# When a two-layer decoder trunk computes its modulation rows: less in the second mixer, more in the feed-forwards

## The chip, the core and the metric

The kernel runs on one core of a Trainium2 chip. A core has five engines with a queue each: PE (TensorE, matrix multiplication, fed by PEld, its weight load), DVE (VectorE), ACT (ScalarE), POOL (GpSimd) and SP (SyncE), which here issues almost every transfer. Each engine takes its queue in order. The metric is the time of one execution on the device in microseconds (us), the median of several runs; lower is better.

## What is computed

A decoder trunk of two layers on 256 tokens of width 2048, in float32. Each layer has a mixer (sliding-window attention beside an RWKV-7 recurrence), an output projection, a LayerNorm, a SwiGLU feed-forward and another LayerNorm. All of it is modulated by six rows per layer, which depend on the conditioning vector `c` alone:

```python
cond = jax.nn.silu(c)
for l in range(DEPTH):
    mod = (jnp.einsum('bd,de->be', cond, w_ada[l]) + b_ada[l]).reshape(B, N_MOD, 1, D_MODEL)
    sh_m, sc_m, gt_m, sh_f, sc_f, gt_f = [mod[:, i] for i in range(N_MOD)]
    u = x * (1 + sc_m) + sh_m
    proj = u @ w_in[l]
    ...            # attention and RWKV-7 groups -> y_attn, y_rwkv
    mix = jnp.concatenate([y_attn, y_rwkv], axis=-1) @ w_out[l]
    x = layer_norm(DEEPNORM_ALPHA * x + gt_m * mix, ln1_w[l], ln1_b[l])
    u = x * (1 + sc_f) + sh_f
    gate, up = jnp.split(u @ w_gate_up[l], 2, axis=-1)
    ffn = (jax.nn.silu(gate) * up) @ w_down[l]
    x = layer_norm(DEEPNORM_ALPHA * x + gt_f * ffn, ln2_w[l], ln2_b[l])
```

A layer's modulation weights `w_ada` are 2048 x 12288 floats, 100 MB: a large part of everything that is read.

## The kernel before

**Weights.** `steps` streams a weight matrix in tiles `raw` of 128x1024 floats (512 KB, four buffers). ACT casts each to `hi`, DVE makes the remainder `lo = raw - hi` (L381; three buffers of `hi`, two of `lo`), and PE multiplies three times: twelve matmuls with 512 columns for a tile in `stream` (L402, L403, L405), or 24 with 256 in `tstream` (L414 to L416).

**Modulation rows.** They are computed on DVE. Two rows of the first layer come at the start; the other ten rows are cut into halves of 1024 columns, 20 half rows in a fixed order, and the generator `ada_steps` computes one in 19 steps: 16 steps each load a tile `ast` (512 KB, two buffers, L253) and add it to `aacc` with one DVE instruction (L255 for the first, L257 for the others); two steps (`LAG`) do nothing; the last sums over partitions (`ada_sums`: eight transposes on PE, L277, and eight sums on ACT, L281). One half row follows another. The six half rows ahead of the second layer's `gt_m` are used by the first layer; the last ones, the second layer's `sc_f`, `sh_f` and `gt_f`, are needed in its feed-forward.

**When a step is taken.** After every weight tile `pump` adds the stage's pace to a counter and takes a step for each whole unit. The recurrence (`recur`, L803 and following) takes `AR` steps ahead of each of its four chunks, each attention operation (a, b, c) takes `AA`. `need` takes all steps that are still missing when a row is used. The paces are per layer: `AP` in the mixer, `AO` in the output projection and up to the first f block of the feed-forward, `AF_` from the second f block on and through the next layer's `front`.

```python
    def pump():
        pace[1] += pace[0]
        while pace[1] >= 1.0:
            pace[1] -= 1.0
            next(ada_rest, None)
...
            for cc in range(NCH):
                adv(AR[l])
...
    for l in range(L):
        pace[0] = AP[l]
```

**The mixer's order.** `ORDER` lists its operations: for four groups of head pairs D (decays), R (projection, `tstream`), A (`prepare`, ends in the products `aa` and `am`), I (`invert`), C (`recur`), E (`close`); Q0 to Q2 project the attention's inputs (`stream`); a, b, c are attention, w and z the output projection's first half. `invert` is a long chain: DVE's `am` goes to memory (`nscr`), comes back as `nb` to POOL, which solves 16x16 triangles with 30 small instructions (L733, L735), goes to memory again (`tinv`) and back as `tm`; DVE transposes it (`ytr`, L745), and PE's products `m` (L749, L756) follow. All these transfers go through SP's one queue.

**Who sets the order.** The program is written in this order, but a planner (a scheduler with a timeline of its own) places each engine's instructions in its queue. So a changed pace also moves other instructions.

Of the kernel before, what the change touches and what calls it, by code (L numbers as in the profile page):

```python
# [45 lines left out]
LAG = 2  # L46
WB = (4, 3, 2)
RED = 1
AR = (3, 7)
AA = (1, 45)  # L50
AP = (0.65, 0.3)
AO = (1.1, 2.9)
AF_ = (0.75, 0.55)
COEX = (0, 0)
IB = 'cb'
EB = 'cb'
# [11 lines left out]
def hybrid_trunk_kernel(  # L68
# [269 lines left out]
    def adv(n):  # L338
        for _ in range(n):
            next(ada_rest, None)  # L340
# [106 lines left out]
    def diagonal(t, rows, row0=0):  # L447

        a = t[:]
        return bass.AP(a.tensor, a.offset + row0 * CH, [[16 * CH + 16, 16 * NCH], [rows * CH, 16 // rows], [1, 16]])  # L450

# [38 lines left out]
    def mixer(l, us, mixp, feeds):  # L490
# [71 lines left out]
        def have_y(kts):  # L562
            for k in kts:
                if ys[k] is None:
                    yf = pool_of("ysc").tile([P, T], F32, tag="ysc", name="yf", bufs=1)
                    dma(yf, yd[l, k])
                    ys[k] = split_y(yf)
# [192 lines left out]
        def recur(g, st):  # L760
# [45 lines left out]
            for cc in range(NCH):  # L806
                adv(AR[l])
                o = cc * P
# [206 lines left out]
        for op in ORDER[l].split():  # L1015
# [31 lines left out]
            if op[0] in "abc":  # L1047
                adv(AA[l])
        have_y(range(KT))
# [65 lines left out]
    def channel(l, ys, wa, fp):  # L1115
# [55 lines left out]
        def affine():  # L1171

            lw = fp.tile([P, D], F32, tag="lnw", name="lnw", bufs=2)
            dma(lw, ln1_w[l:l + 1, :].to_broadcast([P, D]))
            lb = fp.tile([P, D], F32, tag="lnw", name="lnb", bufs=2)
            dma(lb, ln1_b[l:l + 1, :].to_broadcast([P, D]))
            for t in range(2):
                for q in range(4):
                    o = q * 512
                    zq = z[:, t, o:o + 512]  # L1180
                    V.tensor_mul(zq, zq, lw[:, o:o + 512])
                    V.tensor_add(zq, zq, lb[:, o:o + 512])
                    yield
# [14 lines left out]
        for lo_g, hi_g in ((0, 6), (6, 11)):  # L1198
            hts = []
            for f in range(lo_g, hi_g):  # L1200
# [3 lines left out]
                if f == 0:  # L1204
# [4 lines left out]
                    rows = affine()  # L1209
                    pace[0] = AF_[l]  # L1210
                else:
# [103 lines left out]
    for l in range(L):  # L1315
        pace[0] = AP[l]
        with tc.tile_pool(name=f"mix{l}", bufs=1, reuse_waits="tile") as mp:
            ys, wa = mixer(l, us, mp, feeds)
        pace[0] = AO[l]
        with tc.tile_pool(name=f"ffn{l}", bufs=1, reuse_waits="tile") as fp:  # L1320
# [31 lines left out]
```

## Time and profile before

| | |
|---|---|
| three runs | 2698.06 us median (2688.91 to 2700.31) |
| the profiled execution | 2694.28 us |
| its span, first to last instruction | 2692.6 us |
| mean granted TensorE clock | 0.965 of full |

The profile is of one execution. A row of a group list gives count, busy time and the mean of one; a row of waits names who waited and what ended the wait; a timeline row gives start and duration of one instruction or of several merged ones, and in brackets the engine's idle time ahead of it with what ended it. `L381` is line 381 of the kernel.

### The profile page before, as it was taken

The numbers are of one execution on the slowest core, as the hardware profiler recorded it, in microseconds if no ns is written. First come the engines' busy times: TensorE is split into PE (matmuls) and PEld (weight loads), VectorE is DVE, ScalarE is ACT, GpSimd is POOL, SyncE is SP. The second block draws the span as 40 slices with busy tenths as digits, with TensorE's granted clock in tenths as the row PEclk, the third lists the DMA queues.
The fourth block names the chain that finished last, engine by engine and source line by source line (L and its number), as shares of the span: only waits on it lengthen the run. The fifth ranks groups of instructions, "written<-read, shape, count | busy, mean of one in ns | idle before, by whom it ended". The sixth has DMA issues, their size and how long they took to land.

```text
span 2692.6 us, 41752 instructions
## 1 busy us (share of the span) xinstructions
PE 2501.1 (93%) x15325; PEld 2093.1 (78%) x15325; DVE 1841.0 (68%) x2469; ACT 1188.3 (44%) x2029; POOL 135.0 (5%) x355
## 2 busy tenths in 40 slices
PE   3788998788999999999999999979899999999997
PEld 2687886567888888888889877867688888888887
DVE  6866767979877777777788677555764545545456
ACT  2364452435444444444445544534444444344442
POOL 1002112000000000000000022110000000000000
PEclk9789998899999999999999999989999999999999
DMA  9968668688998888889878586424756656666654
GB/s 315 381 188 253 198 191 238 180 317 296 353 330 309 297 303 312 293 295 308 308 263 304 174 259 188 117 72 144 253 172 188 190 186 196 195 189 189 193 188 149
DMA packets 351999, 637.49 MB, mean 237 GB/s; under 512 B 75894, under 2 KB 142898, under 8 KB 350258
## 3 DMA queue, kind: packets, MB, share of 16 engines
q1 hardware_dynamic: 351794, 634.82, 71.6%
q8 instruction: 120, 1.97, 0.3%
q14 instruction: 85, 0.70, 0.1%
HBM read 622.08 MB, written 12.62 MB: 236 GB/s over the span
## 4 chain that ended last, share of the span: by engine, by line
PE 68%; DMA 8%; DVE 6%; ACT 2%; issue 1%; POOL 1%; SPq 0%; DVEq 0%; POOLq 0%; ACTq 0%
PE acc L403 19%; PE acc L402 19%; PE acc L405 19%; DMA ast<-in_w_ada_dram 3%; DVE aacc L257 2%; PE acc L414 2%; PE acc L415 2%; PE acc L416 2%; DVE lo L381 1%; DMA raw<-in_w_gate_up_dram 1%; PE mb L1225 1%; DMA raw<-in_w_out_dram 1%; DMA yf<-yd 1%; PE mb L277 1%; ACT pr L947 0%
## 5 line engine op out<-in xcount | busy, mean ns | idle before, releaser
L380 ACT CAST hi<-raw 128x1024 fp32r<-128x1024 f32 (+2 forms) x728 | 758.5, 1044 | 1110.8 <-PE acc L405 833.1
L381 DVE TENSOR_TENSOR lo<-raw,hi 128x1024 fp32r<-128x1024 f32 (+2 forms) x728 | 880.2, 1212 | 519.8 <-PE acc L403 347.1
L403 PE MATMUL acc<-lo,u 128*128 128x512 f32 x1568 | 513.4, 395 | 11.9 <-DVE lo L381 11.8
L405 PE MATMUL acc<-hi,u 128*128 128x512 f32 x1568 | 505.8, 391 | 0.0
L257 DVE SCALAR_TENSOR_TENSOR aacc<-ast,cond,aacc 128x1024 f32<-128x1024 f32 x300 | 384.1, 1280 | 127.8 <-DMA ast<-in_w_ada_dram 126.6
L402 PE MATMUL acc<-hi,u 128*128 128x512 f32 x1568 | 457.2, 393 | 0.9 <-ACT u L360 0.5
L403 PEld LDWEIGHTS acc<-lo,u 128*128 128x128 f32 x1568 | 293.8, 189 | 76.4 <-DVE lo L381 16.2
L402 PEld LDWEIGHTS acc<-hi,u 128*128 128x128 f32 x1568 | 294.9, 188 | 63.4 <-ACT sg L1218 0.9
L405 PEld LDWEIGHTS acc<-hi,u 128*128 128x128 f32 x1568 | 295.2, 188 | 61.8 <-issue 0.5
L403 PE MATMUL acc<-lo,ht 128*128 128x512 f32 (+1 forms) x720 | 243.6, 377 | 3.0 <-DVE lo L381 2.9
L405 PE MATMUL acc<-hi,ht 128*128 128x512 f32 (+1 forms) x720 | 242.2, 375 | 0.0
L414 PE MATMUL acc<-u,hi 128*128 128x256 f32 x720 | 206.1, 293 | 14.0 <-ACT hi L380 14.0
L402 PE MATMUL acc<-hi,ht 128*128 128x512 f32 (+1 forms) x720 | 217.0, 376 | 0.0
L415 PE MATMUL acc<-u,hi 128*128 128x256 f32 x720 | 204.5, 291 | 0.0
L416 PE MATMUL acc<-u,lo 128*128 128x256 f32 x720 | 193.1, 294 | 7.1 <-DVE lo L381 7.1
L403 PEld LDWEIGHTS acc<-lo,ht 128*128 128x128 f32 x720 | 135.0, 188 | 29.3 <-DVE lo L381 5.6
L414 PEld LDWEIGHTS acc<-u,hi 128*128 128x128 f32 x720 | 141.9, 197 | 19.3 <-ACT hi L380 14.9
L405 PEld LDWEIGHTS acc<-hi,ht 128*128 128x128 f32 x720 | 135.6, 188 | 24.2
L402 PEld LDWEIGHTS acc<-hi,ht 128*128 128x128 f32 x720 | 134.8, 188 | 24.4
L415 PEld LDWEIGHTS acc<-u,hi 128*128 128x128 f32 x720 | 141.7, 197 | 2.6 <-issue 1.6
L416 PEld LDWEIGHTS acc<-u,lo 128*128 128x128 f32 x720 | 133.8, 197 | 11.6 <-DVE lo L381 9.0
L1067 POOL TENSOR_TENSOR brs<-brs,mhalf 128x1 f32<-128x1 f32 x8 | 7.6, 955 | 1698.7 <-DVE brs L1066 772.1
(349 smaller groups left out, 2901.1 us busy)
## 6 DMA issues: line engine op xcount, KB each, us to landing
ast<-in_w_ada_dram SPq DMA_DIRECT2D x368, 512.0 KB
raw<-in_w_gate_up_dram SPq DMA_DIRECT2D x704, 256.0 KB
raw<-in_w_down_dram SPq DMA_DIRECT2D x176, 512.0 KB
raw<-in_w_in_dram SPq DMA_DIRECT2D x82, 512.0 KB
raw<-in_w_out_dram SPq DMA_DIRECT2D x64, 512.0 KB
raw<-in_w_in_dram SPq DMA_DIRECT2D x120, 256.0 KB
ast<-in_w_ada_dram SPq DMA_DIRECT2D x32, 256.0 KB
lnw<-in_ln_w_dram SPq DMA_DIRECT2D x4, 1024.0 KB
```

Source lines behind the costliest of these rows:

```text
L257: ins = V.scalar_tensor_tensor(acc, t, cond[:, j:j + 1], acc, ALU.mult, ALU.add)
L277: PE.transpose(b[:, i * P:(i + 1) * P], blocks[q + i], ident)
L380: S.copy(h, fl)
L381: ins = V.tensor_tensor(r, fl, h.bitcast(F32), ALU.subtract)
L402: PE.matmul(bt, lhsT=xh, rhs=hi[:, c0:c0 + w], start=st, stop=False)
L403: PE.matmul(bt, lhsT=xh, rhs=lo[:, c0:c0 + w], start=False, stop=False)
L405: PE.matmul(banks[t][q][:, 0:w], lhsT=xl, rhs=hi[:, c0:c0 + w], start=False, stop=sp_)
L414: PE.matmul(bt, lhsT=hi[:, c0:c0 + w], rhs=xh, start=st and opens, stop=False)
L415: PE.matmul(bt, lhsT=hi[:, c0:c0 + w], rhs=xl, start=False, stop=False)
L416: PE.matmul(bt, lhsT=lo[:, c0:c0 + w], rhs=xh, start=False, stop=sp_ and closes)
L1067: G.tensor_tensor(rs[:, 0:1], rs[:, 0:1], mhalf[:, 0:1], ALU.pow)
L1225: PE.transpose(b[:, i * T + t * P:i * T + (t + 1) * P], hh[t][:, (2 * k2 + i) * P:(2 * k2 + i + 1) * P], ident)
```

## The change

Four of the tables that set the steps get other numbers for the second layer, and one for the first (`AF_[0]`); the rest of the kernel is untouched.

```diff
-AR = (3, 7)
-AA = (1, 45)
-AP = (0.65, 0.3)
-AO = (1.1, 2.9)
-AF_ = (0.75, 0.55)
+AR = (3, 0)
+AA = (1, 0)
+AP = (0.65, 0.2)
+AO = (1.1, 0.0)
+AF_ = (0.8, 0.55)
```

In the first layer's feed-forward a step now follows 0.8 of the weight tiles, not 0.75. In the second layer's mixer, no steps are taken in the recurrence and in attention, and one follows every fifth weight tile. What is left is taken from the second feed-forward's second f block on. Up to that point of the first feed-forward the two programs are the same.

Three places of the new order. The first is DVE in the second layer's mixer, between group 0's `am` and the first use of its inversion (`bv` frees the bank of a product, `xr` and `lw` prepare groups 1 and 2). Before:

```order
L381 TENSOR_TENSOR lo<-raw,hi 128x1024
L257 SCALAR_TENSOR_TENSOR aacc<-ast,cond,aacc 128x1024
L381 TENSOR_TENSOR lo<-raw,hi 128x1024
L257 SCALAR_TENSOR_TENSOR aacc<-ast,cond,aacc 128x1024
L720 TENSOR_TENSOR bv<-bnb,vx 128x256
L455 SCALAR_TENSOR_TENSOR xr<-acc,par_132,xr 128x255
L608 TENSOR_SCALAR lw<-lw 128x256 x2
L609 SCALAR_TENSOR_TENSOR lw<-rmask,lw 128x256 x2
```

The same place now:

```order
L381 TENSOR_TENSOR lo<-raw,hi 128x1024 x2
L257 SCALAR_TENSOR_TENSOR aacc<-ast,cond,aacc 128x1024
L720 TENSOR_TENSOR bv<-bnb,vx 128x256
L455 SCALAR_TENSOR_TENSOR xr<-acc,par_132,xr 128x255
L381 TENSOR_TENSOR lo<-raw,hi 128x1024
L608 TENSOR_SCALAR lw<-lw 128x256 x2
L609 SCALAR_TENSOR_TENSOR lw<-rmask,lw 128x256 x2
```

The `aacc` between the `lo` are gone but for one; from there to the end of group 1's inversion no other stands. On PE, 82 matmuls with 512 columns and 44 with 256 stood between group 0's last `aa` and its first `m` (L749), and now 72 and 31; the small products between are the same.

The second place is DVE in the LayerNorm that ends the first feed-forward, behind the last `lo` (`tp`, `z`, `bst`: the two halves' residual and statistics; L1078 writes a half's normalised `z`). Before:

```order
L257 SCALAR_TENSOR_TENSOR aacc<-ast,cond,aacc 128x1024
L1264 TENSOR_TENSOR tp<-acc,gtf 128x512
L1265 SCALAR_TENSOR_TENSOR z<-z,tp 128x512
L1267 BN_STATS bst<-z 128x6
L1064 BN_AGGR bmv<-bst 128x2
L1066 TENSOR_SCALAR brs<-bmv 128x1
L1072 SCALAR_TENSOR_TENSOR brs<-bmv,brs 128x1
L1078 TENSOR_SCALAR z<-z,brs 128x512 x2
L1264 TENSOR_TENSOR tp<-acc,gtf 128x512
L1265 SCALAR_TENSOR_TENSOR z<-z,tp 128x512
L1267 BN_STATS bst<-z 128x6
L1064 BN_AGGR bmv<-bst 128x2
```

Now, behind an `aacc` and the first `tp` that stand ahead as before:

```order
L257 SCALAR_TENSOR_TENSOR aacc<-ast,cond,aacc 128x1024
L1265 SCALAR_TENSOR_TENSOR z<-z,tp 128x512
L1267 BN_STATS bst<-z 128x6
L1064 BN_AGGR bmv<-bst 128x2
L1066 TENSOR_SCALAR brs<-bmv 128x1
L1264 TENSOR_TENSOR tp<-acc,gtf 128x512
L1072 SCALAR_TENSOR_TENSOR brs<-bmv,brs 128x1
L1265 SCALAR_TENSOR_TENSOR z<-z,tp 128x512
L1078 TENSOR_SCALAR z<-z,brs 128x512 x2
L257 SCALAR_TENSOR_TENSOR aacc<-ast,cond,aacc 128x1024
L1267 BN_STATS bst<-z 128x6
L257 SCALAR_TENSOR_TENSOR aacc<-ast,cond,aacc 128x1024
```

Three `aacc` have come into it.

The third place is SP's queue in the second layer's mixer, where attention begins: group 3's inversion (`nscr`, `nb`, `tinv`, `tm`), the last projection's result on its way through memory (`qkv`, `qk`) and weights. Before:

```order
L686 DMA nscr<-am 64x4x64 x4
L727 DMA nb<-nscr 64x16x16 x2
L372 DMA raw<-in_w_out_dram 128x1024 x3
L738 DMA tinv_154<-ttl 64x8x16 x2
L372 DMA raw<-in_w_out_dram 128x1024
L876 DMA qkv<-stg 128x512
L372 DMA raw<-in_w_out_dram 128x1024
L741 DMA tm<-tinv_154 64x8x64
L876 DMA qkv<-stg 128x512
L741 DMA tm<-tinv_154 64x8x64
L888 DMA qk<-qkv 128x2x256
```

Now:

```order
L686 DMA nscr<-am 64x4x64 x2
L727 DMA nb<-nscr 64x16x16 x2
L372 DMA raw<-in_w_out_dram 128x1024
L876 DMA qkv<-stg 128x512
L372 DMA raw<-in_w_out_dram 128x1024
L876 DMA qkv<-stg 128x512
L738 DMA tinv_154<-ttl 64x8x16
L888 DMA qk<-qkv 128x2x256
L889 DMA qk<-qkv 128x2x64
L890 DMA vt<-qkv 128x2x64 x2
L738 DMA tinv_154<-ttl 64x8x16
```

The inversion's `tinv` has come behind both `qkv` and stands around the first `qk`. On PE, 55 matmuls with 512 columns stood between group 3's last `aa` and the projection's end, and now 17.

## Rows read from the trace of the kernel before

**Rows 1.** The page's head: each engine's busy time, share, instructions.

```profile
PE 2501.1 (93%) x15325; PEld 2093.1 (78%) x15325; DVE 1841.0 (68%) x2469; ACT 1188.3 (44%) x2029; POOL 135.0 (5%) x355
```

**Rows 2.** Busy time by stretches: length, each engine's busy us, granted clock, DMA share, GB/s.

```profile
700.00:1390.00 690.00, 684.68 (x3159) 566.71 (x3158) 527.29 (x505) 304.38 (x447) 0.00 (x0) 1.00 0.89 308
...
1540.00:1660.00 120.00, 108.37 (x989) 90.53 (x988) 90.25 (x125) 55.26 (x116) 32.55 (x67) 0.94 0.78 235
1660.00:1760.00 100.00, 100.00 (x1083) 84.61 (x1082) 57.15 (x97) 46.65 (x93) 19.80 (x64) 1.00 0.46 126
1760.00:1860.00 100.00, 82.54 (x790) 62.52 (x789) 59.04 (x191) 42.13 (x129) 4.42 (x6) 0.85 0.21 63
1980.00:2640.00 660.00, 660.00 (x2956) 546.85 (x2955) 336.23 (x313) 275.06 (x285) 0.00 (x0) 1.00 0.61 193
```

**Rows 3.** Waits of PE, 1540 to 1660 us: total us, times, longest.

```profile
PE acc L403 <- DVE lo L381: 7.5, 2, 5.3
PE ab L599 <- DVE e L611: 3.0, 1, 3.0
```

**Rows 4.** Timeline of DVE: two of its three longest waits for `ast`.

```profile
1568.95 1.28 DVE L257 SCALAR_TENSOR_TENSOR aacc<-ast,cond,aacc 128x1024 f32<-128x1024 f32 x1 [4.93 <-DMA ast<-in_w_ada_dram]
...
1650.65 1.28 DVE L257 SCALAR_TENSOR_TENSOR aacc<-ast,cond,aacc 128x1024 f32<-128x1024 f32 x1 [6.86 <-DMA ast<-in_w_ada_dram]
```

**Rows 5.** Waits of SP's queue, 1540 to 1670 us.

```profile
SPq L738 <- POOL el L614: 8.4, 1, 8.4
```

**Rows 6.** Stretches of 10 us; the last three columns are clock, DMA share, GB/s.

```profile
1590.00:1600.00 10.00, 10.00 (x122) 9.43 (x122) 7.98 (x12) 6.84 (x24) 0.00 (x0) 0.80 1.02 345
1650.00:1660.00 10.00, 4.68 (x15) 3.71 (x14) 7.71 (x15) 2.35 (x5) 2.57 (x1) 0.66 0.71 194
```

**Rows 7.** Timelines and chain: the inversions of groups 0, 1 and 2.

```profile
1548.76 1.71 PE L681 MATMUL aa<-ar,bkc 64*128 64x128 f32 x16
1563.65 0.44 POOL L733 TENSOR_TENSOR tmp<-nb,ttl 128x15 f32<-128x15 f32 x1 [40.52 <-DMA nb<-nscr]
...
1571.61 1.12 POOL L735 TENSOR_TENSOR ttl<-ttl,tmp 128x30 f32<-128x30 f32 x1
...
1578.95 0.22 POOL L735 TENSOR_TENSOR ttl<-ttl,tmp 128x8 f32<-128x8 f32 x1
...
1588.15 0.71 DVE L745 STREAM_TRANSPOSE ytr<-tm 128x512 f32<-128x512 f32 x1 [0.67 <-DMA tm<-tinv]
1590.25 1.97 PE L749 MATMUL m<-ytr,am 64*64 64x64 f32 x32
...
1668.57 1.08 PE m L749 x32
1674.30 1.09 PE aa L681 x16
1683.45 0.21 POOL L733 TENSOR_TENSOR tmp<-nb,ttl 128x15 f32<-128x15 f32 x1 [24.66 <-DMA nb<-nscr]
...
1694.10 0.22 POOL L735 TENSOR_TENSOR ttl<-ttl,tmp 128x8 f32<-128x8 f32 x1
```

**Rows 8.** Timeline of the first feed-forward's last LayerNorm, DVE and PE.

```profile
1394.36 2.11 DVE L381 TENSOR_TENSOR lo<-raw,hi 128x864 fp32r<-128x864 f32 x2 [0.31 <-ACT hi L380]
...
1406.23 1.53 PE L354 MATMUL mb<-ident,z 128*128 128x128 f32 x6 [4.04 <-DVE z L1078]
```

**Rows 9.** Waits of PE and DVE, 650 to 1400 us.

```profile
PE acc L403 <- DVE lo L381: 6.0, 9, 1.2
...
DVE aacc L257 <- DMA ast<-in_w_ada_dram: 62.2, 52, 3.6
```

**Rows 10.** The chain, where attention begins.

```profile
1760.23 0.25 PE acc L405
...
1769.63 2.32 DMA qk<-qkv
```

**Rows 11.** A stretch of 20 us in the first feed-forward, columns as above.

```profile
720.00:740.00 20.00, 20.00 (x90) 16.53 (x90) 15.98 (x15) 8.34 (x8) 0.00 (x0) 1.00 1.00 370
```

## The prediction

> **What bounds the kernel now.** I read the page's head first: TensorE is busy for 2501.1 us, 93% of the span [rows 1]. That is a mean over unlike stages, so I cut the span into them [rows 2]. The first feed-forward (700 to 1390 us) keeps PE busy 684.68 of 690 us and the second (1980 to 2640) 660 of 660. There only PE's own work counts. The second layer's mixer is different: 108.37 of 120 us in its first part (1540 to 1660), where almost all of its modulation loads lie, 100 of 100 in the next, 82.54 of 100 where attention begins. DVE is busy 90.25 of those 120 us.
>
> Next I read what PE waited for in that first part [rows 3]: DVE's `lo` for 7.5 us in two waits and a bank freed late by DVE for 3.0. DVE's own rows say why it was late [rows 4]: three times, 4.93 us in the first and 6.86 in the last, it stood at the head of its queue on a modulation tile `ast` that had not landed, and the `lo`, `bv` and `e` behind it had to stand too, though they needed nothing of it. The 6.86 us come from SP's queue [rows 5]: its head waited 8.4 us for GpSimd's triangular inversion (`tinv<-ttl`), the `ast` load stood behind that, and DVE got the tile at 1650.65 [rows 4]. After PE's two long gaps the granted clock is below full: 0.80 in the 10 us from 1590, 0.66 in the 10 from 1650 [rows 6].
>
> **What moves.** `pump` runs once per weight tile. From the second f block of the first feed-forward to the end of the next layer's front it runs 80 + 48 + 80 + 40 + 22 = 270 times, so 0.75 to 0.8 adds 13.5, in whole steps 14 (202 to 216). The 20 half rows have 19 steps each (16 loads, LAG 2, one sum), 380 in all, and 138 lie ahead of this stage in both kernels. So the second mixer had 380 - 138 - 202 = 40 steps, of which 28 came from AR (4 x 7 in group 0's recurrence). Now 26 are left, 14 at pace 0.2 in the mixer and 12 in the second feed-forward. In loads, the mixer's 32 become 11; 12 go to the first feed-forward, 9 to the second. AA = 45 and AO = 2.9 found nothing left to give, so their removal does nothing. No load, multiplication or transpose disappears: what can be won is waiting alone.
>
> **Gain: the mixer's first part.** With no `ast` in front of DVE there, the three waits go: 7.5 + 3.0 = 10.5 us [rows 3]. The clock: a mean of 0.94 over 120 us is 14.4 us at the half rate [rows 2], 4.0 of them in the full stretch from 1590; of the 6.8 from 1650 at most 4.68 can have been worked [rows 6]. I take 10 of the 14.4 as worked, which cost half, 5.0, with bounds 2 (after so long a mixer some gap will always come) and 6. Gain 15.5.
>
> **Given back (1): the inversion's latency.** The planner thought DVE full and had put 82 wide and 44 narrow matmuls between group 0's last `aa` and its first `m`; now 72 and 31. By the second feed-forward's pitch (660 us for 2956, 0.22 us, and half of it for a narrow one [rows 2]) that is 3.7 us less cover. The 2.2 and 3.0 us of stall and some 1.7 of the slow clock's cost that also covered the chain are gone: 10.6 us less. The slack was about 0.7 us (`ytr` ends 1588.86, `m` starts 1590.25 [rows 7]). So if the chain stayed as long, PE would wait 9.9 us. But the chain should shrink. From the end of the last `aa` to GpSimd's start it took 13.2 us for group 0, and 8.0 for group 2, which had almost no loads beside it (1550.47 to 1563.65 against 1675.39 to 1683.45 [rows 7]). GpSimd then took 15.5 us (1563.65 to 1579.17) against 10.9 (1683.45 to 1694.32): the same small operation takes 0.22 or 1.12 us [rows 7]. I take 7.5 us of shortening, as weight loads still run: 2.4 us of wait remain, bounds 0 and 9.9. Group 1's `m` came at 1668.57 [rows 7], long after the late `ast` of 1650.65 that its transpose stood behind, so nothing is charged there.
>
> The Trainium skill, SBUF — State Buffer, section "Who interferes with whom", states that a DVE instruction with two SBUF inputs and a GpSimd instruction that reads SBUF block each other for a whole instruction. The trace agrees: the long ones last about as long as a 1.2 us `lo` or `aacc`. By that rule the fewer `aacc` free GpSimd and the wait goes to 0, the sum below to -8.7; with group 0's chain as its rows have it, the wait is 9.9 and the sum +1.2.
>
> **Given back (2): the LayerNorm at the end of the first feed-forward.** The higher pace moves the half row under way: DVE's order now has three more `aacc` between the last `lo` and the last `z` of this LayerNorm. DVE runs there almost without a pause from 1394.36 until PE starts at 1406.23, after 4.04 us on it [rows 8]. Three `aacc` at 1.28 [rows 4] would be 3.84; in the chain rebuilt with the new order some of it falls into DVE's short waits for GpSimd, and the last `z` comes 3.3 us later. Price 3.3 us, bounds 0 (`aacc` slipped into waits) and 6 (a tile that lands late).
>
> **Given back (3): the first feed-forward's body.** Twelve more `aacc` at 1.28 us [rows 4] are 15.4 us on a DVE busy 527 of 690 us [rows 2]. PE there lost 6.0 us in nine waits on `lo`, and DVE waited 62.2 us in 52 waits for `ast` [rows 9]. What hides the additions is the two tiles of `lo` that DVE is ahead. In proportion to the loads that is under 1 us; I take 1.5, bounds 0 and 5. The second feed-forward needs nothing: DVE is busy 336 of 660 us, DMA at 0.61 [rows 2], and a half row's transposes and sums merely move from one full PE stretch to another.
>
> **Given back (4): the start of attention.** In the new order group 3's last `aa` stands 17 wide matmuls ahead of the last projection's end, not 55, and SP's queue puts the first `tinv` ahead of the first `qk` load. Before, `qk` followed the projection's last product by 9.1 us (1760.48 to 1769.63 [rows 10]). Now, from `aa` to the projection's end, 17 wide matmuls take 3.8 us and 38 small ones 2.6 (1.09 for 16 `aa` [rows 7]), so `qk` could start 15.5 us after `aa`; GpSimd, by group 2, ends at 8.0 + 10.9 = 18.9. That is 3.4 us late, partly covered by small products that now fill the same gap: 2.0, bounds -2 and 6.
>
> **Sum.** -15.5 + 2.4 + 3.3 + 1.5 + 2.0 = -6.3. The profiled execution took 2694.28 us (its span of 2692.6 and 1.7 around it): 2688.0. The median shown, 2698.06, lies 3.8 higher, which would give 2691.8; I forecast between the two, **2690**. Its own range is 2683 to 2697. Two runs of this kernel differ by up to 11.4 us, so 0.5% (13.5 us) is about what can be told from no change.
>
> **Rivals.**
> *All is kept:* the chain shrinks fully and the LayerNorm and attention pay nothing: 2694.3 - 15.5 = 2679. For it: the stretch from 1660 to 1760, almost free of loads, has no PE wait at all. Against it: the three `aacc` stand in an unbroken DVE chain.
> *The wait changes its name:* the inversion keeps its length, so 9.9 + 3 us (group 1) come back: -15.5 + 12.9 + 6.8 = +4.2, 2698.5. For it: the 8.4 us that SP waited on GpSimd do not go away by themselves. Against it: group 2.
> *Slower, by the first feed-forward:* there each added step can cost PE its 1.20 us of DVE and the mean wait for its tile, 62.2/52 = 1.20 [rows 9]. It turns the forecast into a loss from three exposed steps of the twelve on; half of them give 2688.0 - 1.5 + 14.4 = 2701, all 2715. For it: while loads run, demand is 1.8 times the weights' own 193 GB/s [rows 2], 347 GB/s, against 338 before. Against it: the twelve loads are 6.3 MB, 20 us at the 308 GB/s of this stage, and its DMA share of 0.89 leaves 76 us of 690 free; and a stretch of 20 us there moved 370 GB/s with PE full throughout [rows 11].
> The Trainium skill, DMA: Bandwidth & Descriptors, section "Where 436 GB/s comes from", gives about 358 GB/s per core as the HBM side's limit; by that rule 347 leaves 3% and hiccups would be paid by PE (an estimate: 17.6 us for the twelve loads, were nothing free). The trace does not bear it out as a limit for one core: that stretch lies above it.
>
> **Chances.** Forecast 0.50, all kept 0.22, wait renamed 0.16, slower 0.12. The range 2676 to 2706 leaves out little more than the far ends of the second and the last. Faster by over 0.5% (below 2684.6): all kept and the forecast's lower edge, 0.26. Slower by over 0.5% (above 2711.5): the last rival's upper part and a term missed, 0.10. Within: 0.64.
>
> **What would show it.** In the new profile: no `aacc` wait of over 3 us between group 0's `aa` and group 1's `m`, and no PE wait on `lo` there; the granted clock at 1.00 in that part; GpSimd's chain of groups 0 and 1 near 11 to 13 us. A PE wait on `ytr` ahead of group 0's `m` measures (1). The wait on `z` at the first feed-forward's end should be near 7 us, not 4. The first feed-forward's PE waits on `lo` should stay below 10 us. The second should be as full as before. I would be wrong if PE's waits there have other owners, a weight tile behind GpSimd in SP's queue above all, or if the planner's new order of other parts costs more than these terms.

## The result, and the profile after

| | median | range, runs |
|---|---|---|
| before | 2693.85 us | 2682.87 to 2700.44, 20 |
| changed | 2701.38 us | 2693.09 to 2711.72, 20 |

The ratio is 1.0029, with a 95% interval of [1.0018, 1.0039]: 5 to 10 us slower, where 8 faster was forecast. That is inside the 0.5% named ahead and inside the range, but on the other side. The profiled executions differ by less, 2692.6 and 2696.7 us of span.

The stretches of [rows 2], now of the changed kernel:

```profile
700.00:1390.00 690.00, 679.13 (x3101) 558.94 (x3100) 531.32 (x500) 302.18 (x449) 0.00 (x0) 1.00 0.90 311
...
1540.00:1660.00 120.00, 117.27 (x1212) 100.67 (x1213) 73.98 (x131) 59.70 (x108) 23.81 (x67) 0.99 0.51 142
1660.00:1760.00 100.00, 99.03 (x989) 83.11 (x987) 55.51 (x85) 48.02 (x94) 13.96 (x43) 1.00 0.55 159
1760.00:1860.00 100.00, 85.40 (x774) 64.61 (x774) 62.53 (x200) 41.46 (x130) 9.70 (x28) 0.85 0.19 58
1980.00:2640.00 660.00, 660.00 (x2960) 546.62 (x2960) 348.13 (x326) 279.25 (x304) 0.00 (x0) 1.00 0.62 200
```

The mixer's first part is what was hoped for: PE 117.27 of 120 us in place of 108.37, the clock 0.99 in place of 0.94. The first feed-forward lost: 679.13 in place of 684.68 us.

Such windows don't move with the program, so I compared the same instruction in both traces: ACT makes the same 784 casts in the same order (L380), and the time from one to another is a stage's length. Casts 140 to 386, counted from 0, are the first feed-forward's body (709.12 to 1388.69 before, 707.65 to 1395.80 now).

| stage (casts) | before | changed | measured | forecast |
|---|---|---|---|---|
| up to cast 140, same program | 709.1 | 707.6 | -1.5 | 0 |
| first feed-forward's body (140 to 386) | 679.6 | 688.2 | +8.6 | +1.5 |
| its LayerNorm (386 to 398) | 29.4 | 31.0 | +1.6 | +3.3 |
| second layer's front (398 to 422) | 83.1 | 85.0 | +1.9 | 0 |
| mixer and attention (422 to 494) | 400.4 | 390.7 | -9.7 | -11.1 |
| output projection, LayerNorm (494 to 518) | 56.1 | 57.2 | +1.1 | 0 |
| second feed-forward's start (518 to 566) | 146.6 | 148.7 | +2.1 | 0 |

The sum is +4.1, the difference of the spans; behind cast 566 nothing moves by more than 0.2. The mixer's gain came nearly as forecast. The first feed-forward took it back.

How much two traces of one program differ can be read from the first row: up to cast 140 all fifteen kernels of this document have the same order of instructions, and that stretch took 703.0 to 715.4 us.

**The first feed-forward.** PE's weight load (PEld) waits for `lo`, 700 to 1396 us, first of the kernel before, then of the changed one:

```profile
PEld acc L403 <- DVE lo L381: 9.9, 13, 1.7
```

```profile
PEld acc L403 <- DVE lo L381: 17.9, 18, 2.1
```

The difference of 8.0 us is nearly the body's loss of 8.6. PE's own rows show less (5.1 and 10.9 us over the same stretch); the ends of matmuls are modelled in this profile. What `lo` is late for stands in DVE's waits and in ACT's (the same stretch, again before and then changed):

```profile
DVE aacc L257 <- DMA ast<-in_w_ada_dram: 62.0, 51, 3.6
ACT hi L380 <- DMA raw<-in_w_gate_up_dram: 18.8, 11, 3.8
ACT hi L380 <- DMA raw<-in_w_down_dram: 11.7, 6, 2.3
```

```profile
DVE aacc L257 <- DMA ast<-in_w_ada_dram: 72.9, 63, 3.9
ACT hi L380 <- DMA raw<-in_w_gate_up_dram: 40.7, 20, 3.8
ACT hi L380 <- DMA raw<-in_w_down_dram: 18.9, 8, 3.0
```

The `ast` waits grew from 62.0 to 72.9 us, and ACT's waits for the weights themselves from 30.5 to 59.6. In both cases there are more waits; the mean `ast` wait stayed at 1.2 us. One such place of the changed kernel, in the timeline of DVE, of ACT and of SP's queue:

```profile
900.66 1.28 DVE L257 SCALAR_TENSOR_TENSOR aacc<-ast,cond,aacc 128x1024 f32<-128x1024 f32 x1 [3.28 <-DMA ast<-in_w_ada_dram]
...
902.99 1.28 DVE L257 SCALAR_TENSOR_TENSOR aacc<-ast,cond,aacc 128x1024 f32<-128x1024 f32 x1
904.19 1.22 DVE L381 TENSOR_TENSOR lo<-raw,hi 128x1024 fp32r<-128x1024 f32 x1
...
910.86 1.28 DVE L257 SCALAR_TENSOR_TENSOR aacc<-ast,cond,aacc 128x1024 f32<-128x1024 f32 x1 [2.79 <-DMA ast<-in_w_ada_dram]
912.06 1.22 DVE L381 TENSOR_TENSOR lo<-raw,hi 128x1024 fp32r<-128x1024 f32 x1
```

```profile
908.29 1.05 ACT L380 CAST hi<-raw 128x1024 fp32r<-128x1024 f32 x1 [1.96 <-DMA raw<-in_w_gate_up_dram]
912.10 1.04 ACT L380 CAST hi<-raw 128x1024 fp32r<-128x1024 f32 x1 [2.76 <-DMA raw<-in_w_gate_up_dram]
```

```profile
904.30 0.33 SPq L253 DMA_DIRECT2D ast<-in_w_ada_dram  x1
905.43 0.80 SPq L372 DMA_DIRECT2D raw<-in_w_gate_up_dram  x2
```

Two kinds of late tile meet: the cast of a weight tile waits for its data, and `lo` stands behind an `aacc` that waits for its own. In the 20 us from 896 PE is busy 17.93.

SP's rows show why the tiles are late: they are asked for late. The `ast` tile that DVE uses at 910.86 was issued at 904.30, as soon as the `aacc` of 902.99 had freed one of the two buffers. The weight tile that is cast at 912.10 was issued at 905.43, as soon as the `lo` of 904.19 had freed one of the four. So it is in the whole body: a load is issued a median of 0.03 us behind the instruction that frees its buffer. Where DVE waits for a modulation tile, it uses the tile a median of 5.2 us after the issue before and 5.25 after the change. Weight tiles that ACT waits for are cast a mean of 5.55 us after theirs before the change and 5.49 after it. The transfers did not become slower. What grew is the number of tiles that DVE is ready for before they land, and such a wait passes through `lo` to the load of the weight tile four further on.

**Its LayerNorm.** PE's wait for the last `z` of [rows 8] went from 4.04 to 4.85, with another of 1.97 ahead of it: 6.8, near the 7 that were named.

```profile
1410.00 0.44 PE L354 MATMUL mb<-ident,z 128*128 128x128 f32 x2 [1.97 <-DVE z L1078]
1415.29 1.54 PE L354 MATMUL mb<-ident,z 128*128 128x128 f32 x6 [4.85 <-DVE z L1078]
```

**Group 0's inversion** [rows 7], GpSimd's first and last instruction, DVE's transpose, PE's wait:

```profile
1562.57 0.21 POOL L733 TENSOR_TENSOR tmp<-nb,ttl 128x15 f32<-128x15 f32 x1 [30.64 <-DMA nb<-nscr]
...
1577.11 0.22 POOL L735 TENSOR_TENSOR ttl<-ttl,tmp 128x8 f32<-128x8 f32 x1
```

```profile
1584.16 0.71 DVE L745 STREAM_TRANSPOSE ytr<-tm 128x512 f32<-128x512 f32 x1 [3.31 <-DMA tm<-tinv]
```

```profile
1584.93 1.73 PE L749 MATMUL m<-ytr,am 64*64 64x64 f32 x32 [2.01 <-DVE ytr L745]
```

The wait is 2.01 us (forecast 2.4). The last `aa` ended at 1554.7, so GpSimd starts 7.9 us behind it (13.2 before, 8.0 forecast) and works 14.8 us (15.5 before; 10.9 in group 2 before).

**The start of attention** [rows 10]: the last projection's matmuls end at 1756.61 and `qk`'s product starts at 1773.25, 16.6 us later; before, it was 13.8 (1760.48 to 1774.28). The difference is 2.8, forecast 2.0.

```profile
1756.22 0.39 PE L405 MATMUL acc<-hi,u 128*128 128x512 f32 x1
...
1773.25 1.37 PE L906 MATMUL acc<-ident,qr 128*128 128x128 f32 x4 [3.34 <-DVE qr L899]
```

**The second feed-forward** now holds a half row's eight transposes, 1.2 us between matmuls on a PE that had no gap:

```profile
2052.60 0.93 PE L277 MATMUL mb<-ident,aacc 128*128 128x128 f32 x7
...
2055.22 0.27 PE L277 MATMUL mb<-ident,aacc 128*128 128x128 f32 x1
```

### The profile page after: what moved, and what is told of

Read it like the earlier page. It is cut to its first block, busy times and chain, and to the rows that moved or that the text cites. A ratio compares the mean times of both kernels' runs of the same rounds, so it can differ in the third digit from the quotient of the medians.

```text
span 2696.7 us, 41738 instructions
## 1 busy us (share of the span) xinstructions
PE 2505.7 (93%) x15325; PEld 2093.7 (78%) x15325; DVE 1841.7 (68%) x2469; ACT 1189.3 (44%) x2029; POOL 125.0 (5%) x355
## 3 DMA queue, kind: packets, MB, share of 16 engines
q8 instruction: 120, 1.97, 0.3%
## 4 chain that ended last, share of the span: by engine, by line
PE 51%; DMA 3%; DVE 3%; ACT 1%; POOL 1%; issue 1%; SPq 0%; DVEq 0%; ACTq 0%; POOLq 0%
PE acc L403 14%; PE acc L402 14%; PE acc L405 14%; PE acc L416 2%; PE acc L414 2%; PE acc L415 2%; DMA ast<-in_w_ada_dram 1%; DVE lo L381 1%; DMA raw<-in_w_out_dram 1%; PE mb L1225 1%; POOL ttl L735 0%; DMA qk<-qkv 0%; DVE aacc L257 0%; PE m L749 0%; DMA raw<-in_w_gate_up_dram 0%
## 5 line engine op out<-in xcount | busy, mean ns | idle before, releaser
L380 ACT CAST hi<-raw 128x1024 fp32r<-128x1024 f32 (+2 forms) x728 | 758.4, 1044 | 1104.0 <-PE acc L405 805.4
L306 DVE SCALAR_TENSOR_TENSOR aacc<-ast,cond,aacc 128x1024 f32<-128x1024 f32 (+1 forms) x75 | 80.3, 1070 | 11.5 <-DMA ast<-in_w_ada_dram 9.9
```

The costliest lines, as they stand in the source:

```text
L306: V.scalar_tensor_tensor(acc, t[:, j], cond[:, j0 + j:j0 + j + 1], acc, ALU.mult, ALU.add)
L380: S.copy(h, fl)
```

## The experiments

The kernels below are the changed one with the edit shown, unless another base is named. "Body" and "mixer" are the stages of the table above, read from one trace of each kernel; the ratio, with its 95% interval, is to the kernel before, and comes from several runs. Three kernels at pace 0.75 (the kernel before and two below) have one order of instructions in the body and took 679.6, 678.9 and 680.2 us there; three at 0.80 have the changed kernel's and took 688.2, 687.0 and 685.4. So less than 3 us between two bodies says little, and the loss is 7.3 us by the means of three.

### Which part costs, which gains

Pace 0.75 kept, the mixer as changed:

```diff
-AF_ = (0.8, 0.55)
+AF_ = (0.75, 0.55)
```

> The change without its higher pace in the first feed-forward (0.75 stays): the second mixer still takes few steps, and the 26 that are left go to the second feed-forward. Theory A (the first feed-forward's extra loads make its weight tiles late, worth about +8 us in its body and +3 to +5 in the LayerNorm and front behind it; the emptier mixer gains about 10): about 10 us faster than the changed kernel and 4 to 9 us faster than the kernel before, no more of PE's waits on lo in the first feed-forward than before (8 us, not 14). Theory B (the emptier mixer gains nothing, because the planner's new order gives all back at the start of attention, and the loss has nothing to do with the pace): as slow as the changed kernel, +5 to +9 us against before.

2698.12 against 2697.31 us, ratio 0.9998 [0.9985, 1.0012]: no change. The body is 678.9 us (before 679.6) and its PEld wait as before, so the loss in the first feed-forward goes with the pace. But the mixer is 399.5 us, hardly shorter than before. Group 0's chain from `aa` to `m` took 30.5 us there, nearly as in the changed kernel (30.3), yet PE waited 5.3 us on `ytr`: the planner had put less other work beside it. That is 3.3 of the 8.9 us between the two mixers; the rest is not traced. Theory A is right on the pace and missed the mixer.

The higher pace alone, on the kernel before:

```diff
-AF_ = (0.75, 0.55)
+AF_ = (0.8, 0.55)
```

> The higher pace in the first feed-forward alone (0.8); the second mixer keeps its tables, and so takes what is left, 26 steps where it had 40. Theory A: the +8 us in the first feed-forward's body and +3 to +5 behind it stand, and the mixer's 14 fewer steps give back a part only: +4 to +10 us against before, PE's waits on lo near 14 us between 640 and 1400. Theory B: the pace costs nothing, 0 to -4 us.

2727.48 us, 1.0104 [1.0087, 1.0122], far worse than either theory had it. The body is 685.4 us (+5.8). Most of the rest is the mixer, 424.1 us: with AR = 7 and only 26 steps left, sixteen `aacc` stand between 1597 and 1646, and group 1's `aa` comes at 1667.92, where it stood at 1608 before. The later groups slip with it, and attention finds group 3's inversion unfinished:

```profile
1667.92 1.16 PE L681 MATMUL aa<-ar,bkc 64*128 64x128 f32 x16
```

```profile
1800.20 0.47 PE L906 MATMUL acc<-ident,qr 128*128 128x128 f32 x1 [10.41 <-DVE qr L899]
```

The change's two halves belong together: under a pace of 0.8 the old mixer tables would have cost 20 us more than the new ones do.

The pace lowered instead:

```diff
-AF_ = (0.8, 0.55)
+AF_ = (0.7, 0.55)
```

> As the change, but the first feed-forward's pace goes down, 0.70 in place of 0.80: 188 steps in place of 216 there, 40 in the second feed-forward. Theory A, if the loss is proportional to the loads: the body gains as much again, 15 to 20 us faster than the changed kernel, 8 to 14 faster than before. Theory A with a threshold (0.75 was still hidden): equal to the kernel with 0.75 and the same tables, within 3 us. Theory B: as the changed kernel.

2686.45 us, 0.996 [0.9945, 0.9976]. The body is 673.3 us (145 tiles, PEld's wait 4.9), the mixer 386.9; the second feed-forward's start costs 6.4 more than before, with 40 steps in it. The body goes on gaining below 0.75, so 0.75 is no threshold: theory A in proportion to the loads.

No step in the mixer at all, pace 0.75:

```diff
-AP = (0.65, 0.2)
+AP = (0.65, 0.0)
-AF_ = (0.8, 0.55)
+AF_ = (0.75, 0.55)
```

> Pace 0.75 in the first feed-forward as before, no step at all in the second mixer, 40 in the second feed-forward (2 of them at once where its rows are needed). Theory A: the last three half-empty loads of the mixer are worth little: within 4 us of the kernel with 0.75 and pace 0.2, so 3 to 10 us faster than before; each half row that goes into the second feed-forward costs about 1 to 3 us there. Theory B: +5 us or more against before.

2681.95 us, 0.9942 [0.9923, 0.996], the best of all: the body 680.2 us, the mixer 381.2, the second feed-forward's start 4.6 longer than before. The mixer is 18 us under that of the kernel with pace 0.2 there, where 4 were expected.

The same with the change's pace:

```diff
-AP = (0.65, 0.2)
+AP = (0.65, 0.0)
```

> The change with pace 0.0 in place of 0.2 in the second mixer: its 14 steps go to the second feed-forward (26 there). It differs from the kernel without mixer steps only by 0.80 for 0.75 in the first feed-forward. If the terms add (body and LayerNorm +10 at 0.80, the mixer without loads 19 us shorter, 2 us for each half row in the second feed-forward): 6 to 12 us slower than that kernel, 3 to 9 faster than before. If the planner's order decides the mixer anew with each shift of the steps: anything from that to slower than before, and the mixer (casts 422 to 494) not within 4 us of 381.

2703.53 us, 1.0026 [1.0012, 1.0039]: as slow as the changed kernel. The body is 687.0 us, as for the other kernels at 0.80 (688.2, 685.4). The mixer has no modulation load in it either, and yet it takes 392.4 us, not 381.2. So a mixer free of loads is not by itself worth 19 us: between 381 and 392 what differs is the planner's order. (The one pair of kernels here that nearly share an order there, two of those below, differ by 2.3 us: 383.7 and 386.0.)

### Bytes or DVE's time

One load of 16 less, DVE's work kept:

```diff
+            if l == 1 and j == 8 and (mod, c0) != (5, 1024):
+                V.scalar_tensor_tensor(acc, acc, cond[:, j:j + 1], acc, ALU.mult, ALU.add)
+                yield
+                continue
```

> The changed kernel without one of the 16 loads of each half row of the second layer (all but the last half row): the step adds the row sum to itself with an instruction of the same length on DVE, so its modulation rows are other numbers. That takes 11 loads of 512 KB away, about as many as the higher pace brings into the first feed-forward, and no instruction of DVE. From the first LayerNorm's end (first transpose of z) to the second's, the kernel before and two others with pace 0.75 took 764.9 to 766.7 us, the two with 0.80 775.5 and 774.3. Theory A1 (the bytes: the weight tiles come later because the engines that move data are full): 765 to 768 here, and ACT's waits for weight tiles near 35 us, not 64. Theory A2 (DVE's time): 774 to 776. In all: A1 about 8 us under the changed kernel, near the kernel before; A2 as the changed kernel, +5 to +10 against before.

2701.04 us, 1.0017 [1.0004, 1.0031]. From LayerNorm to LayerNorm 771.5 us, between the theories; the body 682.9, 5.3 less than the changed kernel and 2.5 less than the shortest body of its order. Lines stand four lower in this kernel:

```profile
PEld acc L407 <- DVE lo L385: 12.9, 17, 1.5
```

All loads, one multiply-add of 16 cut to 32 columns:

```diff
+                w = 32 if l == 1 and j == 8 and (mod, c0) != (5, 1024) else 1024
-                ins = V.scalar_tensor_tensor(acc, t, cond[:, j:j + 1], acc, ALU.mult, ALU.add)
+                ins = V.scalar_tensor_tensor(acc[:, 0:w], t[:, 0:w], cond[:, j:j + 1], acc[:, 0:w], ALU.mult, ALU.add)
```

> The changed kernel with all its loads, but one of the 16 multiply-adds of each half row of the second layer (all but the last half row) works on 32 of the 1024 columns, so its modulation rows are other numbers: about 1.2 us of DVE less, 11 times, and the same bytes. Theory A1 (bytes): still 773 to 776 us from LayerNorm to LayerNorm, +4 to +10 in all against before. Theory A2 (DVE's time): 765 to 769, about the kernel before.

2703.17 us, 1.0035 [1.0017, 1.0053]; the body 688.3, from LayerNorm to LayerNorm 775.5, as the changed kernel:

```profile
PEld acc L404 <- DVE lo L382: 17.6, 22, 1.6
```

Some 12 us less of DVE bought nothing, with only two of DVE's 503 instructions in another place. Theory A2 falls.

Load and multiply-add both left out:

```diff
+            if l == 1 and j == 8 and (mod, c0) != (5, 1024):
+                yield
+                continue
```

> The changed kernel with one of the 16 steps of each half row of the second layer (all but the last half row) left out whole, load and multiply-add, so its modulation rows are other numbers; the pace and all other steps stay. With the load alone gone, the first feed-forward's body (ACT's casts number 140 to 386, counted from the start) took 682.9 us, with the multiply-add alone shortened 688.3, before 679.6, changed 688.2. If bytes and DVE's time add up, 679 to 681 here; if the 3 us that are left belong to where the steps fall (the same steps, other weight tiles), 682 to 684. In all: +0 to +5 against before.

2692.27 us, 0.9989 [0.9975, 1.0003], but the body is still 685.9 us, above both guesses:

```profile
PEld acc L406 <- DVE lo L384: 15.9, 19, 1.5
```

It has 156 tiles and 156 multiply-adds, just as the kernel before with 679.6. So with equal bytes and equal DVE work, where the steps fall among the weight tiles is worth up to 6 us. DVE's order shows one difference: at 0.75 three weight tiles in a row mostly have a multiply-add behind them, at 0.80 four.

Two loads of 16 less, DVE's work kept:

```diff
+            if l == 1 and j in (5, 11) and (mod, c0) != (5, 1024):
+                V.scalar_tensor_tensor(acc, acc, cond[:, j:j + 1], acc, ALU.mult, ALU.add)
+                yield
+                continue
```

> The changed kernel without 2 of the 16 loads of each half row of the second layer (all but the last half row); the step adds the row sum to itself with a DVE instruction of the same length, so its modulation rows are other numbers. In the first feed-forward's body (ACT's casts 140 to 386) the kernel before moves some 147 such loads, the changed one 156, with one load fewer per half row 147, here 137. So far the body was 669 to 671 us plus the time that PE's weight load waits for lo (9.9 us before, 17.9 changed, 12.9 with one load fewer). If bytes set the lateness: below the kernel before, 675 to 679 us, the wait 5 to 9. If the place of the steps sets most of it: 682 or more, the wait 12 or more.

2686.73 us, 0.9974 [0.9963, 0.9985]; the body 675.9, below the kernel before, though DVE still has the changed kernel's 166 instructions. (The loads of the body, each half row's first one counted, are 156 before, 166 changed, 155 with one fewer and 147 here, more than the expectation says.) The planner moved other instructions too: in the body about 110 of DVE's 503 stand elsewhere than in the changed kernel, and 35 with one load fewer.

```profile
PEld acc L407 <- DVE lo L385: 6.1, 10, 1.3
```

The other way round, on the kernel before: each tile number 8 also written to memory.

```diff
             t = adap.tile([P, 1024], F32, tag="ast", name="ast", bufs=2)
             dma(t, src[:, j, n0:n0 + 1024])
+            if l == 1 and j == 8 and (mod, c0) != (5, 1024):
+                dup = dram.tile([P, 1024], F32, name=f"dup{mod}_{c0}")
+                nc.gpsimd.dma_start(out=dup, in_=t)
```

> The kernel before, in which one of the 16 loaded tiles of each half row of the second layer (all but the last half row) is also written back to memory on GpSimd's otherwise idle queue: 11 times 512 KB more moved, about 10 of them in the first feed-forward, no instruction of DVE and no step more; nothing that is computed changes. If bytes set the lateness: the body 684 to 690 us in place of 679.6, the weight load's wait on lo 14 to 20 us, 5 to 10 us slower in all. If the number and place of the steps set it: 678 to 682 us, the wait 9 to 12.

2708.23 us, 1.0058 [1.0041, 1.0075]; the body 694.7 in place of 679.6, with the steps and DVE's instructions of the kernel before (some 25 of 492 in another place). PEld's wait, and one of SP's queue:

```profile
PEld acc L406 <- DVE lo L384: 22.6, 21, 3.1
SPq L253 <- DMA dup<-ast: 34.2, 9, 6.6
```

This test is not one of bytes alone. A tile that is being written out keeps its `ast` buffer, and the load that takes the buffer next stood at the head of SP's queue until the write had ended: nine writes in the body, nine waits, 34.2 us, and the weight loads behind it stood too.

At pace 0.80, 166, 155 and 147 loads give 688.2, 682.9 and 675.9 us, some 0.6 us a load. That fewer loads shorten the body is shown: 12.3 us for 19 of them is more than the 6 us that a placement was worth. That they do it by their bytes, on DMA engines that are full, is not: a load left out also takes away a turn of the two `ast` buffers. The traces speak for the buffers. With two loads fewer, DVE still used a tile that it waited for a median of 5.1 us after its issue (5.25 in the changed kernel), but waited 44.6 us in all, not 72.9. An estimate: two buffers with 5.2 us to land and 1.3 us of use give a tile every 3.3 us, and weight tiles come every 2.8 (679.6/246), so DVE falls behind when many in a row have a step. A third `ast` buffer would decide it; no run has one.

### Other places for the steps

```diff
-AP = (0.65, 0.2)
-AO = (1.1, 0.0)
-AF_ = (0.8, 0.55)
+AP = (0.65, 0.0)
+AO = (1.1, 0.7)
+AF_ = (0.7, 0.55)
```

> Pace 0.70 in the first feed-forward, none in the second mixer, and 0.7 in the second layer's output projection and first f block, so that nothing is taken at once where the rows are needed. If the loads in the mixer cost what the kernel without them suggests (19 us less in the mixer) and the pace 0.70 gives 4 us in the first feed-forward, it is the best so far: 16 to 24 us faster than before, 2674 to 2682 on this frame. If the gain of the kernel without mixer steps was the planner's luck with one order: 5 to 12 us.

2685.61 us, 0.9957 [0.9943, 0.9971]. Body 672.1 and mixer 379.8 are the best pair of all, but the output projection and its LayerNorm take 67.1 us, not 56.1: there PE waits for DVE's `z`, and steps are now taken there.

```profile
PE mb L1100 <- DVE z L1078: 10.0, 1, 10.0
```

With AO = 1.25 and AF_ = 0.65:

> As the last, with 0.65 in the first feed-forward and 1.25 in the output projection. The step from 0.80 to 0.75 took 9.4 us from LayerNorm to LayerNorm, that from 0.75 to 0.70 4 us. Theory A1 with a floor (the body is full of PE's own work below 0.70): 1 to 2 us less than at 0.70 there, given back in the output projection, whose DMA share was 0.65: within 4 us of the last kernel. Proportional to loads: 4 us less again.

2701.95 us, 1.0023 [1.001, 1.0036]. The body stays at 672.1 (136 tiles; 144 in the last kernel), so the floor is reached, and the output projection with its LayerNorm takes 83.2.

Steps in attention:

```diff
-AA = (1, 0)
-AP = (0.65, 0.2)
-AF_ = (0.8, 0.55)
+AA = (1, 1)
+AP = (0.65, 0.0)
+AF_ = (0.72, 0.55)
```

> Pace 0.72 in the first feed-forward, none in the second mixer's weight tiles, 12 steps in its attention (one for each operation), 36 in the second feed-forward. In the kernel without mixer steps the attention's stretch from 1800 to 1850 moves 85 GB/s and DVE is not full there. If loads are cheap where nothing else is moved: mixer 381 to 385 us, body 3 to 5 us under 679.6, in all 16 to 22 us faster than before. If DVE's multiply-adds stand before attention's own work (maxima, exponentials' sums): the mixer 388 or more, 5 to 10 us faster than before.

2688.37 us, 0.9972 [0.996, 0.9985]. The mixer is 390.5: from L530's first matmul to the last projection's end it took 265.8 us (264.2 in the kernel without mixer steps), and `qk` came 23.0 us behind that in place of 16.8. So the loss is at the start of attention, as the second theory has it; that the multiply-adds are its cause was not traced. The body is 682.5 with 150 tiles, more than at 0.75. The traced execution, 2694.53 us, is the slowest of twelve, and no second trace has this order, so the cause stays open.

## Why the prediction was wrong

**The failed step is (3), the first feed-forward's body**: 1.5 us with bounds of 0 and 5, measured 8.6. Two things in it were wrong. It read the slack from PE's waits on `lo` (6.0 us, in nine), where the weight load's waits (9.9) are what the length follows: in every kernel here the body is 668 to 673 us plus PEld's wait on `lo`, from 672.1 with 2.7 to 694.7 with 22.6. And it scaled that wait "in proportion to the loads". Loads grew by 6% (156 to 166) and the wait by 81%. The two `lo` tiles of lead that were to hide the additions don't bridge a wait of 3 us for `ast` with a weight tile late beside it.

The runs show that the number of loads is a cause (fewer of them, the pace kept) and that DVE's time is not one (the shortened multiply-adds). They don't split the loss: taking the added loads away gave back 5.3 us with the `aacc` left in place and 2.3 without, where bodies of one order differ by up to 2.8. Where the steps fall is worth as much: 156 tiles took 679.6 in one placement and 685.9 in another. Why a step costs what it does is not settled by a run. By the traces the tiles take as long from issue to use in both kernels and are asked for late, so the turn of the two `ast` buffers is the nearest reason; transfers that grew slower are not seen.

The rival "slower, by the first feed-forward", given 0.12, had the right place and about half its price. Its turning point was a little off: an `aacc` takes 1.28 us, not 1.20, and three exposed steps (7.4 us) would not yet have made up 6.3 + 1.5; it takes a fourth. The DMA share of 0.89, which it had against it, said nothing on this: spare time on the DMA engines does not help a load that is issued late. The changed kernel's GB/s over 700 to 1390, in forty slices of 17 us, ahead of it the DMA share in tenths:

```profile
DMA  8998999989679999988898899969998999699978
GB/s 295 366 342 267 396 330 321 319 298 341 236 247 316 326 326 320 333 287 288 299 363 293 289 313 328 346 212 316 358 325 258 345 325 329 230 327 350 328 263 288
```

The Trainium skill, DMA: Bandwidth & Descriptors, section "Where 436 GB/s comes from", gives about 358 GB/s as the memory side's limit of a core. By it the loss was to come in this stage, and it did. But a slice at 396 shows that 358 is not a ceiling in this trace, the loss comes at a mean of 311, and the times from issue to use show no slower transfers.

**Gain and (1).** The three waits went as forecast, the clock rose to 0.99, and the remaining wait is 2.0 us against 2.4. From the first matmul of L530 (1478.59 before, 1489.29 now) to the last projection's end it is 267.3 us, not 281.9: -14.6, forecast -13.1. That the wait was so close is partly luck. GpSimd's part shrank by 0.7 us only (group 2 had suggested 4.6), the way to it by 5.3, and the way from its end to `ytr`'s, on which nothing was forecast, by 2.2 (9.7 before, 7.5 now). In all that is 8.2 us, where 7.5 was taken. And the slack that was read as 0.7 us is 1.4 by its own rows (1588.86 to 1590.25). With both put right the same sum gives 10.6 - 1.4 - 8.2 = 1.0.

The Trainium skill, SBUF — State Buffer, section "Who interferes with whom", holds every DVE instruction with two SBUF inputs against a GpSimd instruction that reads SBUF. `lo` is one as well. That fits the traces: in the two kernels with no `aacc` in the whole mixer GpSimd still took 13.0 and 14.0 us for group 0. No run here takes the `lo` away.

But the kernel with pace 0.75 had the same tables in the mixer and gained 0.9 us there, and the two without any load there took 381.2 and 392.4. That the gain came as forecast is partly the planner's order for this one set of numbers.

**(2)** was 3.3, measured 1.6 in that stage. The front behind it, which had no term, took 1.9 more; in the traces it goes with the pace (82.0 to 83.5 us at 0.75, 85.0 to 86.2 at 0.80). **(4)** was 2.0, measured 2.8.

**The second feed-forward** "needs nothing" was wrong by 2.1 us. The transposes did not move from one full PE stretch to another: in the mixer PE had gaps for them, here it had none. One half row cost 2.0 to 2.1 us at its start in three kernels, two half rows 4.6 and 6.4.

**What would have been seen.** Of the signs named, the waits on `lo` in the mixer (0.8 us left), the clock (0.99) and the `z` wait came as said, and GpSimd's chain did for group 1 (10.9 us) but not for group 0 (14.8, where 11 to 13 was named). The limit set for the first feed-forward, PE's `lo` waits below 10 us, was broken by 10.9. That was the sign for the loss.

## What to carry to other kernels

In a stage that PE fills, read the weight load's waits, not only PE's, and don't scale them in proportion: 6% more loads cost 81% more waiting. When an operand is late, ask first when its load was issued and which buffer it waited for; only then whether the transfer was slow. Moving loads out of a stalled stage pays only if they go where nothing is near its limit. Here the second feed-forward came nearest to that (pace 0.75, none in the mixer, 0.9942), where a half row costs 2 to 3 us; the first feed-forward and the output projection both charged more. And where a planner orders the program, a few steps more or less reshuffle distant parts by 10 to 25 us, so compare several neighbouring settings before a gain is put down to a mechanism.

## What had not been expected of the hardware

A tile of 512 KB written to memory from GpSimd's queue held up SP's queue by 3.8 us on average (34.2 us in nine waits), because the next load needed its buffer; a queue of its own did not make the write free. The DMA share in the first feed-forward is nearly the same in both kernels, 0.89 and 0.90, while PE's loss there almost doubled: the share does not show the lateness, the waits do.
